# Prologue of a decoder step: the stores of memory keys, values and fold products issued from ScalarE's queue instead of SyncE's

## The chip, the core and the metric

The kernel runs on one core of one Trainium2 chip. The metric is device time in microseconds (us) of one execution, as the median of several runs. The engines are named as the profile names them: PE is TensorE (matmuls), PEld its weight loads, DVE is VectorE, ACT is ScalarE, POOL is GpSimd, and SP is SyncE, which computes nothing and here issues every transfer. A DMA is issued by an instruction in some engine's queue; the transfer itself then runs on 16 DMA engines that all queues share.

## What is computed

One layer of a decoder trunk for 2048 prompt tokens and 64 sample tokens: a combined input projection, sliding-window attention and a pooling mixer, an output projection, cross-attention into 256 memory tokens, a squared-ReLU MLP, and a final norm. All is float32 at the interface, model width 1024. The part that matters here is the memory:

```python
def _mem_kv(mem, g_mem, w_ck, w_cv):
    hm = _rmsnorm(mem, g_mem)
    k = (hm @ w_ck).reshape(B, N_MEM, N_CROSS_HEADS, CROSS_HEAD_DIM)
    v = (hm @ w_cv).reshape(B, N_MEM, N_CROSS_HEADS, CROSS_HEAD_DIM)
    return k, v
...
    q = (h @ w_cq).reshape(B, L, N_CROSS_HEADS, CROSS_HEAD_DIM)
    s = jnp.einsum('blhd,bmhd->bhlm', q, mem_k).astype(jnp.float32) * (CROSS_HEAD_DIM ** -0.5)
    p = jax.nn.softmax(s, axis=-1)
    o = jnp.einsum('bhlm,bmhd->blhd', p.astype(mem_v.dtype), mem_v).reshape(B, L, D_MODEL)
    x = x + o @ w_co
```

The memory keys and values of the prompt are also outputs.

## The kernel before

Precision comes from splitting each float32 operand in a rounded high part and a low rest, and from three matmuls per product (`mm3`, lines 108 to 113): high by high, high by low, low by high. A weight therefore passes through four steps in `Stream.emit` (lines 126 to 139): a load of 512 KB into one of six float32 buffers `f`, a cast by ACT into a high tile `w` (L136), a subtraction into a low tile `w` (L137, mostly DVE), and then the buffer is free for the next load. Twelve `w` tiles hold six weights.

The kernel has a prologue and three superblocks of 768, 768 and 576 tokens. The prologue (`prologue`, lines 368 to 452) runs once:

1. Memory keys and values: 8 + 8 weights (`in_wck`, `in_wcv`), each 24 matmuls of 256 columns. `evac` (from line 392) scales a result by the memory norm on DVE (L394), stores it to `out_mk` or `out_mv`, and splits it with `rnd` (ACT L96, DVE L97).
2. Key folds: the query weight is multiplied into the keys once, 8 weights `in_wcqt`, each giving two results of 128 x 512. `put_fold` (lines 336 to 341) copies a result from PSUM into an `f` buffer (ACT L338) and stores it to the DRAM tensor `a_s`.
3. Value folds: for each of 4 heads two weights `in_wco` give four results of 128 x 512, stored to `b_s` by the same helper.
4. The pooling weight is folded into the output weight (`prep_fold`, `fold`): the weight `in_wpool` is scaled by ACT L350 and DVE L351, and eight results go to `wo_s`. This stands between matmuls of the first superblock's input projection (L286 to L288).

Between these steps stand the first norms of the two 384-token blocks of superblock 0 (`norm1`): squares on ACT (L207, L210), their sum on POOL (L211), a column sum on PE (L220), a reciprocal root (ACT L223, L224, DVE L225 to L227), and the scaled and split activations (DVE L238, ACT L239, DVE or POOL L241).

`f` buffers are handed out when the program is written, and the copies of `put_fold` use the same six as the weight loads. In the folds, two of them serve all weight loads in turn (`f_93` and `f_96`, later `f_93` and `f_92`), and four hold results. The order of the instructions on each engine is set before the run by a scheduler that estimates durations; every engine then works its queue strictly in that order. PSUM has four buffers `mm` for these results, so a matmul group waits for the copy of the result four groups before it.

Of the kernel before, what the change touches and what calls it, by code (L numbers as in the profile page):

```python
# [51 lines left out]
def kernel(ctx: ExitStack, tc: tile.TileContext, io, nW=12, nF=6, nT=8):  # L52
    nc = tc.nc
# [37 lines left out]
    def f32(ap):  # L91
        return ap.bitcast(F32)

    def rnd(ps, hi, lo, scale=None):
        if scale is None:
            nc.scalar.copy(hi, ps)  # L96
            nc.vector.tensor_tensor(lo, ps, f32(hi), ALU.subtract)  # L97
        else:
            nc.scalar.activation(hi, ps, AF.Copy, scale=scale)
            nc.vector.scalar_tensor_tensor(lo, ps, scale, f32(hi), ALU.mult, ALU.subtract)  # L100
# [4 lines left out]
    def w8(t):  # L105
        return t[:].rearrange("p (k c) -> p k c", c=P)

    def mm3(ps, ks, Wh, Wl, Hh, Hl, first=True, final=True):
        last = len(ks) - 1
        for i, k in enumerate(ks):  # L110
            nc.tensor.matmul(ps, Wh(k), Hh(k), start=first and i == 0, stop=False)  # L111
            nc.tensor.matmul(ps, Wh(k), Hl(k), start=False, stop=False)  # L112
            nc.tensor.matmul(ps, Wl(k), Hh(k), start=False, stop=final and i == last)  # L113
# [195 lines left out]
    def flush(all_=False):  # L309
        for x in list(later):  # L310
            x[0] -= 1
            if all_ or x[0] <= 0:
                later.remove(x)
                g = x[1]()
                if g is None:
                    continue
                if all_:
                    run(g)
                elif next(g, 1) is None:
                    later.append([1, lambda g=g: g])  # L320
# [15 lines left out]
    def put_fold(ps, dsts):  # L336
        o = FS.get()
        nc.scalar.copy(o[:, 0:512], ps)  # L338
        for dst, src in dsts(o):
            nc.sync.dma_start(dst, src)  # L340
        FS.put(o)

    def prep_fold():
# [11 lines left out]
    def fold(g, wpr):  # L355
        th, tl = S.next(("wop", g))
        for eh in range(2):
            ps = MM.get()
            mm3(ps[:], [0], lambda k: wpr[:, P * g:P * g + P], lambda k: wpr[:, 512 + P * g:512 + P * g + P],
                lambda k: th[:, 512 * eh:512 * eh + 512], lambda k: tl[:, 512 * eh:512 * eh + 512])  # L360
            put_fold(ps[:], lambda o: [(wo_s[4 * eh:4 * eh + 4, :, P * g:P * g + P].rearrange("e p c -> p e c"),
                                        o[:, 0:512].rearrange("p (e c) -> p e c", c=P))])
            MM.put(ps)
        WS.put(th, tl)
        if g == 3:
            WS.put(wpr)

    def prologue():
        S.resW, S.resF = 1, 0
        mx = [XT[1][:, 0:1024], XT[1][:, 1024:2048]]  # L370
        mem = lambda k: mx[k // 4][:, 256 * (k % 4):256 * (k % 4 + 1)]
        warm = AUX.get()
        for _ in range(14):
            wu = nc.tensor.matmul(warm[:, 0:P], ones[:], ident[:], start=True, stop=True)
        AUX.put(warm)
        nc.sync.dma_start(vec[:], io["vec"])
        nc.sync.dma_start(mx[0][:, 0:512], io["mem"][:, 0:512])
        S.emit()
        hm = Act(256)
        nm = Norm(256, mem, add=nc.vector)  # L380
        for i in range(4):
            if i:
                nc.sync.dma_start(mx[i // 2][:, 512 * (i % 2):512 * (i % 2) + 512], io["mem"][:, 512 * i:512 * (i + 1)])
            for k in range(2 * i, 2 * i + 2):
                g = vec[:, V_GMEM + k:V_GMEM + k + 1]
                nc.scalar.activation(hm.hi(k), mem(k), AF.Copy, scale=g)
                nc.vector.scalar_tensor_tensor(hm.lo(k), mem(k), g, f32(hm.hi(k)), ALU.mult, ALU.subtract)
        S.emit()
        for k in range(8):
            nm.sq(k)  # L390
        S.pump()
        def evac(a, dst, c, ps):
            t = TS.get()
            nc.vector.tensor_tensor(t[:, 0:256], ps[:, 0:256], nm.r[:, 0:256], ALU.mult)  # L394
            MM.put(ps)
            nc.sync.dma_start(dst[:, 256 * c:256 * (c + 1)], t[:, 0:256])
            rnd(t[:, 0:256], a.hi(c), a.lo(c))
            TS.put(t)

        pend, outs = [], []  # L400
        for name, dst in (("ck", io["mk"]), ("cv", io["mv"])):
            a = Act(256)
            outs.append(a)
            for c in range(8):
                th, tl = S.next((name, c))
                ps = MM.get()
                if name == "ck" and c == 0:
                    with tc.issue_after(wu.ins):
                        mm3(ps[:, 0:256], range(8), lambda k: w8(th)[:, k, :], lambda k: w8(tl)[:, k, :], hm.hi, hm.lo)
                else:  # L410
                    mm3(ps[:, 0:256], range(8), lambda k: w8(th)[:, k, :], lambda k: w8(tl)[:, k, :], hm.hi, hm.lo)
                WS.put(th, tl)
                pend.append((a, dst, c, ps))
                if name == "ck" and c == FINC:
                    nm.fin()
                if name == "cv" or c >= FINC:
                    while pend:
                        evac(*pend.pop(0))
                flush()
                if (name, c) == N1C:  # L420
                    norm1(blk[0][0], N1W)
        TS.put(nm.r)
        hm.free()
        mk, mv = outs
        norm1(blk[0][1], N1Q)
        for c in range(8):
            th, tl = S.next(("cq", c))
            for hf in range(2):
                ps = MM.get()
                for h2 in range(2):  # L430
                    ks = [(hf * 2 + h2) * 2, (hf * 2 + h2) * 2 + 1]
                    mm3(ps[:, 256 * h2:256 * h2 + 256], ks, lambda k: w8(th)[:, k, :], lambda k: w8(tl)[:, k, :], mk.hi, mk.lo)
                put_fold(ps[:], lambda o: [(a_s[hf, c // 2, :, 512 * (c % 2):512 * (c % 2) + 512], o[:, 0:512])])
                MM.put(ps)
            WS.put(th, tl)
            flush()
        mk.free()
        for h in range(4):
            w = [S.next(("co", 2 * h)), S.next(("co", 2 * h + 1))]
            for mb in range(2):  # L440
                for eh in range(2):
                    ps = MM.get()
                    mm3(ps[:], range(2),
                        lambda k: mv.hi(2 * h + k, mb * P, mb * P + P), lambda k: mv.lo(2 * h + k, mb * P, mb * P + P),
                        lambda k: w[k][0][:, 512 * eh:512 * eh + 512], lambda k: w[k][1][:, 512 * eh:512 * eh + 512])
                    kt = h * 2 + mb
                    put_fold(ps[:], lambda o: [(b_s[4 * eh:4 * eh + 4, :, P * kt:P * kt + P].rearrange("e p c -> p e c"),
                                                o[:, 0:512].rearrange("p (e c) -> p e c", c=P))])
                    MM.put(ps)
                flush()  # L450
            WS.put(*w[0], *w[1])
        mv.free()
# [13 lines left out]
    def norm1(bl, wait=2):  # L466
        n = bl.n
        if bl.s == 0:
            xs = []
            load_x(bl)  # L470
            nm = Norm(n, bl.x)
        else:
            xs = [FS.get() for _ in range(4)]
            for i in range(4):
                nc.sync.dma_start(xs[i][:, 0:2 * n], io["x"][:, 8 * bl.t0 + 2 * i * n:8 * bl.t0 + 2 * (i + 1) * n])
            nm = Norm(n, lambda k: xs[k // 2][:, n * (k % 2):n * (k % 2) + n])
        for k in range(8):
            nm.sq(k)

        def rest():  # L480
            nm.fin()
            bl.h1 = Act(n)
            yield from nm.apply(V_GMIX, bl.h1.hi, bl.h1.lo, PIECE0 if bl.s == 0 else PIECE[0][bl.b])
            FS.put(*xs)

        later.append([wait, rest])
# [864 lines left out]
```

## Time and profile before

| | us |
|---|---|
| median of 3 runs | 2626.17 (2624.62 to 2628.29) |
| the profiled execution's own time | 2623.82 |
| its span, first to last instruction | 2622.0 |
| PE busy in the span | 2562.3 |
| ACT busy | 982.8 |
| DVE busy | 1300.5 |
| stores of `put_fold` | 40, of 256 KB each, issued from 67.5 to 141.4 us |
| stores of `evac` | 16, of 128 KB each, issued from 24.4 to 63.7 us |

The span and the busy times are of one profiled execution. A row of a timeline view gives start, duration, engine, line, operation, output and inputs, a count, and in brackets the idle time before it with what ended it. A waits view sums such idle times by the line that waited and the line that it waited for (total, times, longest).

### The profile page before, as it was taken

What the parts mean: (1) busy time and instruction counts of PE and PEld (TensorE: products, weight loads), DVE (VectorE), ACT (ScalarE), POOL (GpSimd) and SP (SyncE); (2) the same over time, 40 slices, a digit from 0 to 9 for tenths busy, and PEclk for the clock granted to TensorE, in tenths of its full rate; (3) what the DMA queues carried; (4) which work ended last, traced back from release to release, by engine and by line L of the source; (5) the groups of instructions that cost most, each with busy time, mean ns of one, the idle gap of its engine ahead of it and who ended that gap; (6) DMA issues with size and microseconds to landing.
All of it is one profiled execution on the core that took longest, in us unless ns stands there. A gap on an engine that the chain in (4) does not pass through costs nothing. (4 is left out here: it accounts for less than half of the span.)

```text
span 2622.0 us, 39268 instructions
## 1 busy us (share of the span) xinstructions
PE 2562.3 (98%) x15753; PEld 2457.1 (94%) x15753; DVE 1300.5 (50%) x2283; ACT 982.8 (37%) x1923; POOL 657.9 (25%) x723
## 2 busy tenths in 40 slices
PE   9899999999999999999999999999999999999998
PEld 8799989999999999897999999999999669999998
DVE  8567453533333367936363333334765645344334
ACT  6666342422222244824342222223464444322231
POOL 2215322411111152433241111113334214111111
PEclk9999999999999999999999999999999999999999
DMA  7833111211221123131111211112414572222210
GB/s 280 263 122 117 62 49 51 86 61 63 65 65 65 57 73 106 57 120 57 65 64 65 65 60 62 65 57 70 145 58 149 184 278 100 81 82 88 82 57 37
DMA packets 92539, 244.76 MB, mean 93 GB/s; under 512 B 16772, under 2 KB 31556, under 8 KB 91204
## 3 DMA queue, kind: packets, MB, share of 16 engines
q1 hardware_dynamic: 92356, 242.25, 27.9%
q8 instruction: 123, 2.02, 0.3%
q14 instruction: 60, 0.49, 0.1%
HBM read 219.53 MB, written 22.69 MB: 92 GB/s over the span
## 5 line engine op out<-in xcount | busy, mean ns | idle before, releaser
L286 PE MATMUL mm<-act,w 128*128 128x384 f32 (+2 forms) x2784 | 901.1, 324 | 2.8 <-ACT act L642 1.6
L287 PE MATMUL mm<-act,w 128*128 128x384 f32 (+2 forms) x2784 | 897.0, 322 | 3.4 <-POOL act L241 1.5
L288 PE MATMUL mm<-act,w 128*128 128x384 f32 (+2 forms) x2784 | 895.6, 322 | 1.4 <-DVE w L137 1.4
L136 ACT CAST w<-f 128x1024 fp32r<-128x1024 f32 x330 | 344.3, 1049 | 702.7 <-PE mm L112 457.6
L137 DVE TENSOR_TENSOR w<-f,w 128x1024 fp32r<-128x1024 f32 x330 | 418.4, 1276 | 305.7 <-ACT w L136 304.8
L111 PE MATMUL mm<-act,w 128*128 128x384 f32 (+2 forms) x1728 | 552.3, 320 | 2.8 <-DVE t L394 2.2
L113 PE MATMUL mm<-act,w 128*128 128x384 f32 (+2 forms) x1728 | 548.8, 318 | 1.9 <-DVE w L137 1.9
L112 PE MATMUL mm<-act,w 128*128 128x384 f32 (+2 forms) x1728 | 548.5, 317 | 0.0
L287 PEld LDWEIGHTS mm<-act,w 128*128 128x128 f32 x2784 | 525.7, 189 | 12.7 <-POOL act L241 3.7
L286 PEld LDWEIGHTS mm<-act,w 128*128 128x128 f32 x2784 | 525.8, 189 | 7.6 <-issue 2.3
L288 PEld LDWEIGHTS mm<-act,w 128*128 128x128 f32 x2784 | 525.6, 189 | 2.2 <-DVE w L137 2.0
L1144 POOL TENSOR_TENSOR t<-t 128x384 f32<-128x384 f32 (+2 forms) x192 | 216.4, 1127 | 1038.6 <-ACT t L1143 1038.6
L1177 DVE TENSOR_TENSOR x<-mm,x 128x384 f32<-128x384 f32 (+2 forms) x384 | 199.7, 523 | 327.5 <-PE mm L113 327.5
L111 PEld LDWEIGHTS mm<-act,w 128*128 128x128 f32 x1728 | 326.8, 189 | 4.7 <-ACT t L207 2.4
L113 PEld LDWEIGHTS mm<-act,w 128*128 128x128 f32 x1728 | 326.8, 189 | 2.4 <-DVE w L137 2.3
L112 PEld LDWEIGHTS mm<-act,w 128*128 128x128 f32 x1728 | 326.9, 189 | 1.1 <-issue 0.3
L211 POOL TENSOR_TENSOR t<-t,t 128x384 f32<-128x384 f32 (+2 forms) x161 | 182.2, 1132 | 337.0 <-ACT t L210 329.6
L1147 DVE TENSOR_TENSOR act<-t,act 128x384 fp32r<-128x384 f32 (+2 forms) x192 | 101.4, 528 | 295.5 <-ACT act L1146 295.4
L1146 ACT CAST act<-t 128x384 fp32r<-128x384 f32 (+2 forms) x192 | 93.5, 487 | 233.6 <-POOL t L1144 233.6
L210 ACT ACTIVATE t<-x 128x384 f32<-128x384 f32 (+2 forms) x140 | 68.0, 498 | 161.7 <-DVE x L1105 74.5
L111 PE MATMUL mm<-w,act 128*128 128x512 f32 x288 | 116.5, 407 | 9.7 <-ACT w L136 9.7
L1143 ACT ACTIVATE t<-mm 128x384 f32<-128x384 f32 (+2 forms) x192 | 88.3, 460 | 92.5 <-PE mm L288 88.6
(187 smaller groups left out, 2216.9 us busy)
## 6 DMA issues: line engine op xcount, KB each, us to landing
f<-in_wup SPq DMA_DIRECT2D x96, 512.0 KB, 3.5
f<-in_wdn SPq DMA_DIRECT2D x96, 512.0 KB, 3.5
f<-in_win SPq DMA_DIRECT2D x30, 512.0 KB, 3.8
f<-a_s SPq DMA_DIRECT2D x24, 512.0 KB, 3.5
f<-b_s SPq DMA_DIRECT2D x24, 512.0 KB, 4.7
x<-in_x SPq DMA_DIRECT2D x6, 1536.0 KB, 6.9
f<-in_wco SPq DMA_DIRECT2D x16, 512.0 KB, 5.4
f<-in_cmk SPq DMA_DIRECT2D x16, 512.0 KB, 4.3
```

Of the source, the lines that this page charges most:

```text
L111: nc.tensor.matmul(ps, Wh(k), Hh(k), start=first and i == 0, stop=False)
L112: nc.tensor.matmul(ps, Wh(k), Hl(k), start=False, stop=False)
L113: nc.tensor.matmul(ps, Wl(k), Hh(k), start=False, stop=final and i == last)
L136: nc.scalar.copy(th[:], r[:, 0:1024])
L137: eng.tensor_tensor(tl[:], r[:, 0:1024], f32(th[:]), ALU.subtract)
L211: self.add.tensor_tensor(self.acc[:, 0:n], self.acc[:, 0:n], t[:, 0:n], ALU.add)
L286: nc.tensor.matmul(ps[:, 0:n], w8(th)[:, k, :], hi(b, k), start=k == 0, stop=False)
L287: nc.tensor.matmul(ps[:, 0:n], w8(th)[:, k, :], lo(b, k), start=False, stop=False)
L288: nc.tensor.matmul(ps[:, 0:n], w8(tl)[:, k, :], hi(b, k), start=False, stop=k == 7)
L1144: nc.gpsimd.tensor_tensor(q[:, 0:n], r[:, 0:n], r[:, 0:n], ALU.mult)
L1147: nc.vector.tensor_tensor(lo, q[:, 0:n], f32(hi), ALU.subtract)
L1177: nc.vector.tensor_tensor(bl.x(m), ps[:, 0:n], bl.x(m), ALU.add)
```

## The change

All 56 stores named above are issued from ACT's queue. In `evac` the store also moves behind the split, so that it stands after ACT's cast. Nothing else is edited.

```diff
@@ put_fold
         nc.scalar.copy(o[:, 0:512], ps)
         for dst, src in dsts(o):
-            nc.sync.dma_start(dst, src)
+            nc.scalar.dma_start(dst, src)
@@ evac
             MM.put(ps)
-            nc.sync.dma_start(dst[:, 256 * c:256 * (c + 1)], t[:, 0:256])
             rnd(t[:, 0:256], a.hi(c), a.lo(c))
+            nc.scalar.dma_start(dst[:, 256 * c:256 * (c + 1)], t[:, 0:256])
             TS.put(t)
```

SP's queue falls from 509 to 453 rows and ACT's grows from 1587 to 1643. The scheduler also puts other instructions of the prologue in another order. Three places follow; in a row, the tile left of the arrow is written and those right of it are read.

The first place is ACT in the key folds, where the second block's squares meet the sixth `in_wcqt` weight (`w_85`, loaded into `f_96`). Before:

```order
L136 CAST w_85<-f_96 128x1024
L96 CAST act_72<-t_104 128x256
L210 ACTIVATE t_99<-x_106 128x384
L210 ACTIVATE t_98<-x_106 128x384
L338 COPY f_94<-mm_107 128x512
L338 COPY f_95<-mm_108 128x512
L239 CAST act_76<-t_102 128x384
L338 COPY f_91<-mm_109 128x512
L210 ACTIVATE t_104<-x_106 128x384
```

Now:

```order
L338 COPY f_94<-mm_107 128x512
L210 ACTIVATE t_104<-x_106 128x384
L340 DMA a_s<-f_94 128x512
L338 COPY f_95<-mm_108 128x512
L239 CAST act_76<-t_102 128x384
L340 DMA a_s<-f_95 128x512
L136 CAST w_85<-f_96 128x1024
L338 COPY f_91<-mm_109 128x512
L338 COPY f_92<-mm_110 128x512
```

The cast of that weight moved behind the squares, two copies and two stores; the square into `t_104` moved ahead of the copies of `f_95` and `f_91`.

The second place is ACT at the first head of the value folds. `w_85` and `w_87` are here the fourth and fifth `in_wco` weights; the copies of `mm_107` to `mm_110` ahead of the first `b_s` store are head 0's results. Before:

```order
L136 CAST w_85<-f_96 128x1024
L338 COPY f_94<-mm_107 128x512
L338 COPY f_95<-mm_108 128x512
L136 CAST w_87<-f_93 128x1024
L338 COPY f_96<-mm_109 128x512
L338 COPY f_91<-mm_110 128x512
```

Now (the first pair of copies and stores belongs to the last key fold):

```order
L136 CAST w_85<-f_96 128x1024
L338 COPY f_91<-mm_109 128x512
L338 COPY f_92<-mm_110 128x512
L340 DMA a_s<-f_91 128x512
L340 DMA a_s<-f_92 128x512
L239 CAST act_64<-t_101 128x384
L136 CAST w_87<-f_93 128x1024
L338 COPY f_94<-mm_107 128x512
L338 COPY f_95<-mm_108 128x512
L340 DMA b_s<-f_94 128x4x128
L340 DMA b_s<-f_95 128x4x128
```

Head 0's first two copies stood ahead of the cast of `w_87` and stand behind it now. In the same stretch DVE has a new order; `w_84<-f_93` is the low part of the third `in_wco` weight, whose end frees `f_93` for the fifth. Now:

```order
L137 TENSOR_TENSOR w_82<-f_96,w_81 128x1024
L241 TENSOR_TENSOR act_65<-t_97,act_63 128x384
L238 SCALAR_TENSOR_TENSOR t_103<-x_106,vec,t_99 128x384
L238 SCALAR_TENSOR_TENSOR t_104<-x_106,vec,t_99 128x384
L238 SCALAR_TENSOR_TENSOR t_101<-x_106,vec,t_99 128x384
L238 SCALAR_TENSOR_TENSOR t_100<-x_106,vec,t_99 128x384
L238 SCALAR_TENSOR_TENSOR t_98<-x_106,vec,t_99 128x384
L241 TENSOR_TENSOR act_65<-t_103,act_63 128x384
L238 SCALAR_TENSOR_TENSOR t_97<-x_106,vec,t_99 128x384
L137 TENSOR_TENSOR w_84<-f_93,w_83 128x1024
```

Before, three of these eight norm rows stood between the two L137 rows; now all eight do.

The third place is PE at the first pool fold (`w_85` here the first `in_wop` weight, `w_81` the scaled pool weight) within the second group of the input projection (`mm_110`):

```order
 L286 MATMUL mm_110<-act_63,w_83 128x384
 L287 MATMUL mm_110<-act_65,w_83 128x384
+L111 MATMUL mm_108<-w_85,w_81 128x512
+L112 MATMUL mm_108<-w_86,w_81 128x512
+L113 MATMUL mm_108<-w_85,w_81 128x512
+L111 MATMUL mm_109<-w_85,w_81 128x512
+L112 MATMUL mm_109<-w_86,w_81 128x512
+L113 MATMUL mm_109<-w_85,w_81 128x512
 L288 MATMUL mm_110<-act_63,w_84 128x384
```

The fold stood behind 19 matmuls of that group and stands behind 2 now. Behind the value folds, ACT's casts and copies go head by head: the two casts for a later head, then the four copies of a head with their stores.

## The prediction

> **What bounds the kernel now.** I read the page first, then a table by stage, then the waits of PE, of SP and of ACT in the prologue, and last the timelines around the longest waits.
>
> ```profile
> PE 2562.3 (98%) x15753; PEld 2457.1 (94%) x15753; DVE 1300.5 (50%) x2283; ACT 982.8 (37%) x1923; POOL 657.9 (25%) x723
> ```
>
> PE is busy for 98% of the span, so only time in which PE stands still can be won. The change edits the prologue alone, and its stores end at about 142 us. The table by stage has duration, busy time of each engine, granted clock, DMA share and GB/s.
>
> ```profile
> 24.50:66.00 41.50, 41.18 (x338) 40.74 (x338) 37.90 (x55) 28.17 (x52) 17.42 (x15) 1.00 0.72 245
> 66.00:88.70 22.70, 19.97 (x147) 19.33 (x148) 17.48 (x22) 16.39 (x30) 9.95 (x9) 0.92 0.77 261
> 88.70:115.70 27.00, 22.78 (x97) 17.55 (x96) 12.11 (x11) 16.22 (x27) 5.13 (x3) 1.00 0.97 279
> 115.70:127.90 12.20, 11.47 (x62) 10.61 (x61) 6.09 (x11) 8.23 (x16) 0.00 (x0) 1.00 0.86 259
> 127.90:160.00 32.10, 31.27 (x177) 29.97 (x176) 17.91 (x30) 15.48 (x25) 1.17 (x4) 1.00 0.68 220
> ```
>
> Keys and values (first row) keep PE full. The key folds (second row) lose 2.7 us, the value folds (third row) 4.2 us, and there the DMA engines are busy 97% of the time. The largest waits of PE from 24.5 to 130 us name what ended them:
>
> ```profile
> PE mm L111 <- ACT w L136: 3.5, 2, 3.0
> PE aux L220 <- POOL t L211: 2.7, 1, 2.7
> PE mm L111 <- ACT w L350: 0.7, 1, 0.7
> ```
>
> By the table PE stands still for 0.3 + 2.7 + 4.2 + 0.7 = 7.9 us up to 127.9, the most that the change can win but for a slow clock behind L220's wait, which comes below. SP waits a lot, but the question is how long it keeps loads waiting:
>
> ```profile
> SPq L340 <- ACT f L338: 17.7, 14, 3.0
> ...
> 76.78 0.80 SPq L132 DMA_DIRECT2D f<-in_wco  x1
> 81.55 0.41 SPq L132 DMA_DIRECT2D f<-in_wco  x1
> 89.93 0.33 SPq L132 DMA_DIRECT2D f<-in_wco  x1
> 97.42 0.59 SPq L132 DMA_DIRECT2D f<-in_wco  x1
> ```
>
> The 17.7 us of store waits look like loads held back. The last three rows, loads into `f_93`, tell otherwise. Each needs the end of L137 of the weight before it in that buffer:
>
> ```profile
> 79.14 1.22 DVE L137 TENSOR_TENSOR w<-f,w 128x1024 fp32r<-128x1024 f32 x1 [3.36 <-ACT w L136]
> 88.69 1.21 DVE L137 TENSOR_TENSOR w<-f,w 128x1024 fp32r<-128x1024 f32 x1
> 95.93 1.23 DVE L137 TENSOR_TENSOR w<-f,w 128x1024 fp32r<-128x1024 f32 x1 [1.02 <-ACT w L136]
> ```
>
> The ends 80.36, 89.90 and 97.16 stand against issues at 81.55, 89.93 and 97.42: SP is late by 1.2, 0.03 and 0.26 us. What the loads mostly wait for is the buffer, and that comes back over a chain of load, cast and subtraction. The casts of that chain, and its last link, the scaled pool weight:
>
> ```profile
> 94.85 1.05 ACT L136 CAST w<-f 128x1024 fp32r<-128x1024 f32 x1 [0.72 <-DMA f<-in_wco]
> 103.12 1.05 ACT L136 CAST w<-f 128x1024 fp32r<-128x1024 f32 x1 [0.75 <-DMA f<-in_wco]
> 111.26 1.05 ACT L136 CAST w<-f 128x1024 fp32r<-128x1024 f32 x1
> 118.67 1.05 ACT L136 CAST w<-f 128x1024 fp32r<-128x1024 f32 x1 [0.28 <-DMA f<-in_wop]
> 123.64 1.28 ACT L350 ACTIVATE w<-f,vec 128x128 fp32r<-128x128 f32 x4 [0.60 <-DMA f<-in_wpool]
> ```
>
> A link takes 8.27, 8.14 and 7.41 us: 2.33 from the cast's start to the end of L137, and the rest the load. The issue rows from 66 to 125 us have the time from issue to landing last:
>
> ```profile
> b_s<-f SPq DMA_DIRECT2D x16, 256.0 KB, 5.6
> ...
> f<-in_wpool SPq DMA_DIRECT2D x1, 256.0 KB, 2.6
> ...
> DMA to landing us min/median/max: 4.0/4.9/6.8
> ```
>
> The last row is of the weight loads in that stretch. So the value folds are bound by a transfer's time over two buffers, with the DMA engines nearly full.
>
> **The change part by part.** Each edit is costed with these rows.
>
> The 16 stores of keys and values. They leave SP, so the loads behind them go earlier; PE stands still for only 0.3 us in 41.5 there, so this wins at most that. On ACT each issue stands behind a cast and may run beside it. I take 0.
>
> The column sum L220. The second block's squares are added on POOL, and PE waits in order for the sum:
>
> ```profile
> 68.08 1.02 POOL L241 TENSOR_TENSOR act<-t,act 128x384 fp32r<-128x384 f32 x1
> 69.06 5.64 POOL L211 TENSOR_TENSOR t<-t,t 128x384 f32<-128x384 f32 x4
> 74.75 1.19 PE L220 MATMUL aux<-t,ones 128*128 128x384 f32 x2 [2.66 <-POOL t L211]
> 76.00:77.00 1.00, 1.00 (x6) 1.00 (x6) 0.00 (x0) 0.00 (x0) 0.63 (x1) 0.50 0.85 285
> 79.00:80.00 1.00, 1.00 (x10) 1.00 (x10) 0.86 (x1) 0.97 (x3) 0.00 (x0) 1.00 1.10 391
> ```
>
> In the new order the square into `t_104` comes earlier and that L241 behind the sums, so the last four adds can start about 1.8 us sooner (1.02 for the L241, and 0.8, my choice, for the square), at 67.2, and end at 72.9. PE waits 0.8 instead of 2.66, and the granted clock of 0.50 that follows (6 matmuls in a us against 10) should not come. Gain here: 1.9 of the wait, and about 1.1 of the slow clock. Bounds: 0 and 3.8.
>
> Its loss at head 1. The value folds' second head needs head 0's first copy to free its PSUM buffer. That copy now stands behind the cast of the fifth `in_wco` weight. The third weight's L137, which frees its buffer, now stands behind eight norm rows. They are like these:
>
> ```profile
> 82.13 1.68 DVE L238 SCALAR_TENSOR_TENSOR t<-x,vec,t 128x384 f32<-128x384 f32 x3
> ```
>
> The second weight's load goes out at 76.78 at the latest, lands 4.9 later, and cast and L137 take 2.33: 84.0. Eight rows of 0.56 are 4.5, the L137 behind them 1.2, so it ends at 89.7, as before (89.90), though its own cast is earlier. The load, issued at 89.8, lands at 94.7; the cast ends at 95.75 and the copy, 0.55, at 96.3. Head 1 began at 94.01:
>
> ```profile
> 94.01 0.39 PE L111 MATMUL mm<-w,act 128*128 128x512 f32 x1
> ```
>
> So it starts 2.3 us later, whatever was won at L220; PE has merely stood still here instead. What counts is the chain's cast, at 94.7 against 94.85.
>
> The links from there. SP's lateness is gone, 0.3 us in all, and I take the median of 4.9 for a load: three links of 2.33 + 4.9 give 116.4 for the cast that was at 118.67, 2.3 earlier. Bounds for a load: 4.0 and 6.8, the ends of that row.
>
> The issues on ACT. No trace row has a DMA issued from ACT; the nearest are SP's own (minimum, median and maximum in ns):
>
> ```profile
> L340 SPq DMA_DIRECT2D a_s<-f x16: 319/375/1132, 67.5 to 90.6; - x16
> L340 SPq DMA_DIRECT2D b_s<-f x16: 359/432/1560, 93.7 to 116.6; - x16
> ```
>
> For one head ACT has two casts (2.1), four copies (2.1 at 0.53) and four issues. At 0.43 each that is 5.9 us in a link of 7.2, which the load's flight covers. Bounds: 0.32 and 1.56 an issue; above 0.75 the cover is gone.
>
> The tail. The first matmuls of the input projection need head 3's first copy, now behind the cast at 116.4: 116.4 + 1.05 + 0.55 = 118.0, where they began at 115.72.
>
> ```profile
> 115.72 0.33 PE L286 MATMUL mm<-act,w 128*128 128x384 f32 x1
> 119.91 0.33 PE L286 MATMUL mm<-act,w 128*128 128x384 f32 x1
> 124.09 0.50 PE L111 MATMUL mm<-w,w 128*128 128x512 f32 x1 [0.72 <-ACT w L350]
> ```
>
> Twenty-four of them take 4.19, so 0.175 each. The pool fold comes after 26 of them, at 122.55; the pool weight is ready at 116.4 + 2.33 + 2.6 + 1.28 = 122.6. So the fold starts at 122.6, 1.5 earlier than 124.09, but 17 matmuls that stood ahead of it then are still to come, 3.0 us. **Sum: 3.0 - 1.5 = 1.5 us later** at the same point of the work. Behind it all is as before, and PE stood still for only 0.8 in the 32 us to 160. On the profiled execution's 2623.82 this gives 2625.3; that execution lay 2.35 below the median, so on the median's scale it is 2627.7.
>
> [...]
>
> **The rivals.**
>
> Shorter loads, faster. With stores no longer ahead of a load in its own queue, a load could take 4.0 each time. Five flights of the sum (the second weight's, the fifth's, three links) then give 4.5 back: 1.5 - 4.5 = -3.0, 2623.2 us. If PE so keeps also the 3.0 won at L220, -6.0, 2620.2 us. For it: the shortest flight in the row is 4.0. Against it: the DMA share of 0.97 with 279 GB/s. [...]
>
> ACT's queue becomes the bound, slower. If an issue from ACT takes 1.13 us, the worst of the `a_s` issues, a head costs ACT 2.1 + 2.1 + 4.5 = 8.7 against a link of 7.2: 1.5 more for each of three heads, 4.6 in all, on top of 1.5: 2632.3. It decides from 0.75 us an issue. A load of 5.6, as long as a `b_s` store, does much the same: five times 0.7 more, 2631.2. For it: full DMA engines, long issues. Against it: the median issues of 0.375 and 0.432.
>
> Nothing moves. SP's lateness was 1.5 us on this chain, most of it ahead of the place where the gain is lost. If the new order's losses and gains cancel, the time stays at 2626.2.
>
> **How the numbers follow.** A measurement of this kernel can tell about 0.2%, 5.3 us, from no change. My forecast, with the rival of nothing moved and the milder part of the others, stays within that: 0.64. Slower by more needs loads over 5.6 us or issues over a microsecond: 0.23. Faster by more needs short loads and the gain at L220 kept: 0.13. The range goes from that case, 2620.2, to loads of 5.6 (+3.5) with half of the dear issues (+2.3) on top of the sum, 2633.5.
>
> **What would show it.** Right: PE's wait at L220 under 1 us and no clock of 0.50 behind it; head 1 starting about 96 behind a cast of `in_wco`; the last cast of the chain near 116.4; the pool fold near 122.6. Wrong: weight loads landing in about 4 us from 90 to 115 us, or ACT's issues well over 0.43 us, or PE standing still in keys and values, where I have it unchanged. If the cast of `w_85`, moved back behind two stores, starved the sixth key fold, the loss would show as PE waiting for L136 near 79.

## The result and the profile after

| | before | after |
|---|---|---|
| median, us (6 runs each, on the same chip) | 2627.49 (2624.62 to 2628.50) | 2634.51 (2631.46 to 2639.16) |
| ratio | | 1.0030, 95% interval 1.0017 to 1.0043 |
| the profiled execution's own time, us | 2623.82 | 2633.56 |
| its span, us | 2622.0 | 2631.8 |

The change makes the kernel 0.3% slower, 7.0 us by the medians. The forecast was 2627.7 with a range up to 2633.5, so the result lies 1.0 beyond the range, on the side of the slower rival.

The page of the changed kernel, then its table by stage (duration, busy time of each engine, granted clock, DMA share, GB/s), with the stretches that were shown of before:

```profile
PE 2567.2 (98%) x15753; PEld 2460.3 (93%) x15753; DVE 1296.2 (49%) x2283; ACT 984.3 (37%) x1923; POOL 652.8 (25%) x723
```

```profile
24.50:66.00 41.50, 41.18 (x338) 40.74 (x338) 36.02 (x54) 27.19 (x47) 14.94 (x15) 1.00 0.69 243
66.00:88.70 22.70, 19.21 (x140) 18.54 (x141) 16.67 (x18) 16.00 (x28) 10.01 (x9) 0.92 0.74 237
88.70:115.70 27.00, 21.92 (x90) 16.66 (x89) 12.42 (x15) 17.76 (x29) 3.70 (x3) 0.94 0.86 270
115.70:127.90 12.20, 10.09 (x44) 9.12 (x43) 3.27 (x5) 5.56 (x12) 0.00 (x0) 0.86 0.74 219
127.90:160.00 32.10, 31.76 (x173) 29.75 (x172) 16.91 (x24) 17.81 (x29) 1.17 (x4) 1.00 0.81 262
```

PE now stands still for 0.3 + 3.5 + 5.1 + 2.1 = 11.0 us up to 127.9, 3.1 more than before. The clock column adds the rest: it falls below 1 in three rows instead of one. The DMA share has fallen from 0.97 to 0.86 in the value folds: the transfers are not what got scarcer. What PE waits for there is new (total, times, longest, from 24 to 130 us):

```profile
PE mm L111 <- ACT f L338: 8.8, 8, 2.6
...
PE mm L286 <- ACT f L338: 2.1, 1, 2.1
```

Before, PE waited for weights (L136) and for the norm's sum. Now it waits for ACT's copies, which free its PSUM buffers; the wait at L220 is gone. The three long ones, in PE's timeline, with the start of the pool fold behind them, and a single microsecond in the form of the stage table:

```profile
68.03 0.44 PE L111 MATMUL mm<-act,w 128*128 128x256 f32 x1 [2.30 <-ACT f L338]
...
106.21 0.79 PE L111 MATMUL mm<-w,act 128*128 128x512 f32 x1 [2.59 <-ACT f L338]
...
121.54 0.45 PE L286 MATMUL mm<-act,w 128*128 128x384 f32 x1 [2.11 <-ACT f L338]
...
128.27 0.39 PE L111 MATMUL mm<-w,w 128*128 128x512 f32 x1
```

```profile
69.00:70.00 1.00, 1.00 (x7) 1.00 (x7) 0.41 (x1) 1.00 (x2) 0.92 (x2) 0.50 0.69 262
```

Each of these waits has a stretch of 3.41 us at half clock (granted 0.50) with it, from 68.22, 105.77 and 122.83, worth 1.7 us. Three such stretches against one before (from 75.25) are two more, 3.4 us; with the 3.1 us of standing still that makes 6.5. It agrees with the pool fold: 4.2 us later than before (128.27 against 124.09), with 29 matmuls of the input projection done ahead of it instead of 43, 14 x 0.175 = 2.5 us still to come, together 6.7. Up to 160 us PE is then as full as before, and the loss stays: the same rows of DVE come 6.9 us later at 170 us and still at 1130 us. The spans of the two profiled executions differ by 9.8 us. The other 2.9 come behind 1130 us, where PE's queue has the same order in both; stretches at half clock fall at other places there. That they have to do with the change is not shown.

### The profile page after: what moved, and what is told of

It is laid out like the page before. It is cut to its first block, busy times and chain, and to the rows that moved or that the text cites. A ratio compares the mean times of both kernels' runs of the same rounds, so it can differ in the third digit from the quotient of the medians.

```text
span 2631.8 us, 39240 instructions
## 1 busy us (share of the span) xinstructions
PE 2567.2 (98%) x15753; PEld 2460.3 (93%) x15753; DVE 1296.2 (49%) x2283; ACT 984.3 (37%) x1923; POOL 652.8 (25%) x723
## 5 line engine op out<-in xcount | busy, mean ns | idle before, releaser
L136 ACT CAST w<-f 128x1024 fp32r<-128x1024 f32 x330 | 344.1, 1049 | 700.4 <-PE mm L112 455.9
L137 DVE TENSOR_TENSOR w<-f,w 128x1024 fp32r<-128x1024 f32 x330 | 418.4, 1275 | 303.1 <-ACT w L136 302.6
L111 PE MATMUL mm<-w,act 128*128 128x512 f32 x288 | 117.2, 409 | 11.3 <-ACT w L136 6.2
```

The source lines that it names most:

```text
L136: nc.scalar.copy(th[:], r[:, 0:1024])
L137: eng.tensor_tensor(tl[:], r[:, 0:1024], f32(th[:]), ALU.subtract)
```

## The experiments

Each was timed against the kernel before in the same round on the same chip, 5 to 12 runs each. "Over before" is the measured ratio less one, times 2627 us, with its 95% interval. It is not the difference of the medians: copies_first_old is 1.8 us over before by its ratio and 3.5 by its medians (2630.97 against 2627.47). So a difference of two us between two rows says little by itself.

| kernel | order of the computing | stores | median, us | over before, us |
|---|---|---|---|---|
| before | old | SP | 2626.5 to 2628.4 | |
| the change | new | ACT | 2634.51 | 7.9 (4.5 to 11.3) |
| new_order_sp | new | SP | 2641.97 | 13.1 (10.0 to 16.3) |
| old_order_act | old | ACT | 2628.52 | 0.8 (-1.6 to 3.2) |
| evac_only | scheduler's | 16 on ACT | 2629.94 | 3.2 (0.8 to 5.3) |
| fold_only | scheduler's | 40 on ACT | 2629.82 | 3.4 (1.1 to 5.5) |
| new_then_old | new, from the value folds old | ACT | 2633.91 | 5.5 (3.2 to 7.9) |
| old_then_new | old, from the value folds new | ACT | 2632.03 | 3.7 (1.3 to 5.8) |
| copies_first | new, two copies moved | ACT | 2632.98 | 5.8 (3.2 to 8.1) |
| copies_first_old | the same, from the value folds old | ACT | 2630.97 | 1.8 (-1.1 to 4.7) |
| cast_first | new, a cast moved | ACT | 2632.89 | 5.0 (2.6 to 7.4) |
| cast_copies_first | new, copies and cast moved | ACT | 2633.32 | 6.0 (3.7 to 8.4) |
| cast_copies_old | the same, from the value folds old | ACT | 2629.88 | 2.1 (0.0 to 4.5) |
| double_issue | old | ACT, folds' in halves | 2641.02 | 12.6 (9.2 to 16.0) |
| late_issue | old | ACT, issued later | 2631.31 | 3.7 (1.3 to 6.0) |
| fix_l220_sp | old, three moves | SP | 2629.00 | 0.8 (-1.3 to 3.2) |
| pool_b | old | 24 on POOL, rest SP | 2667.43 | 41.0 (37.3 to 44.7) |

### The order or the queue

The change does two things at once: it moves the issue of 56 stores, and the scheduler answers with another order on ACT, DVE, POOL and PE. Both can be parted by pinning an order: each instruction of an engine gets an added edge that says "issued behind this one" to its neighbour. So there is a kernel with the old stores and the new order, and one with the new stores and the old order. Their traces have the rows of ACT, DVE and POOL in exactly the order of the changed kernel and of the kernel before.

```python
PIN = {"Activation": [...], "DVE": [...], "Pool": [...], "PE": [...]}   # prologue, places in program order
for e, seq in PIN.items():
    ins = [...]                     # the computing instructions of engine e
    for p0, p1 in zip(seq, seq[1:]):
        tc.add_manual_dep(ins[p1], ins[p0].name, ...NoSync...)
```

> The stores stay on SP, where they were before, and ACT, DVE, POOL and PE work through the prologue in exactly the order of the changed kernel. Theory 'order' (the loss comes from where the new order puts copies, casts and squares on ACT, not from the queue that issues the stores): 4 to 9 us slower than before (the change cost 7.0), with PE waiting 6 us or more for the copies of L338 up to 130 us. Theory 'queue' (the loss comes from ACT's issue instructions, or from the stores' flights out of ACT's queue): within 2 us of before, and PE waiting under 2 us for L338.

> All 56 stores are issued by ACT, and ACT, DVE, POOL and PE work through the prologue in exactly the order of the kernel before; only the issue instructions are new on ACT. Theory 'order': within 2 us of before, PE waiting under 2 us for L338. Theory 'queue': 4 to 9 us slower than before, with PE waiting for L338 or for the squares behind slower stores. If it comes out over 2 us faster, SP's lateness was worth more than the 1.5 us that I read for it.

The order is the loss: with the old order and ACT's stores the time is that of before within the noise, with the new order and SP's stores it is 13.1 us over. PE's largest wait in each, of new_order_sp first:

```profile
PE mm L111 <- ACT f L338: 14.0, 8, 5.1
```

```profile
PE mm L111 <- ACT f L338: 3.8, 5, 1.2
```

The second meets the time that the theory of the order gave it, but not the wait: 3.8 us for copies, where under 2 were expected. The first misses what either theory gave it, by 4 us: the new order is worse with SP than with ACT. The DVE, SP, ACT and PE timelines of new_order_sp show why, around head 2 of the value folds:

```profile
95.92 1.23 DVE L137 TENSOR_TENSOR w<-f,w 128x1024 fp32r<-128x1024 f32 x1 [1.44 <-ACT w L136]
...
99.75 2.34 SPq L340 DMA_DIRECT2D b_s<-f  x4
102.19 8.35 SPq L132 DMA_DIRECT2D f<-in_wco  x3
...
107.88 2.23 ACT L136 CAST w<-f 128x1024 fp32r<-128x1024 f32 x2 [5.87 <-DMA f<-in_wco]
...
110.65 0.79 PE L111 MATMUL mm<-w,act 128*128 128x512 f32 x1 [5.11 <-ACT f L338]
```

A buffer is free at 97.15, but SP still has four stores ahead of the load, each of which waits for a copy that the new order makes late; the load goes out at 102.19, 5.0 us late, and PE stands for 5.1. So the stores' move does what it says, loads no longer wait behind them, and in the new order that is worth 5.2 us (13.1 against 7.9, with intervals that overlap by a little). In the old order, where SP was late by 1.2, 0.03 and 0.26 us, it is worth nothing that can be measured (0.8, -1.6 to 3.2).

Of the 5.0 us by which that load was late, 2.3 are the four issues (99.75 to 102.09); for the rest a store stood at the head of SP's queue and waited for its copy.

### Each edit alone

Only one of the two edits of the diff, with the order that the scheduler then makes.

> The 16 stores of keys and values on ACT, the 40 of the folds on SP. Its order on ACT has the copy of f_94 behind the squares, as in the changed kernel, and head 0's copies ahead of the fifth in_wco cast, as before. Theory 'order': the first part of the loss, 1.5 to 3.5 us, with PE standing still near 68 us for the first fold buffer. Theory 'queue' with the issues of the folds as the cost: within 1 us of before. Theory 'queue' with slower landing of out_mk and out_mv as the cost: 2 to 5 us.

> The 40 stores of the folds on ACT, the 16 of keys and values on SP. Its order on ACT has the fold copies ahead of the square into t_104, and head 0's copies behind the fifth in_wco cast, as the changed kernel has. Theory 'order': no gap near 68 us, the later part of the loss stays, 3 to 5.5 us. Theory 'queue': the whole 7 us if the folds' issues are the cost, within 1 us if the flights of out_mk and out_mv are.

Both came out where the theory of the order had them, 3.2 and 3.4 us. The waits of PE from 66 to 130 us, of evac_only first:

```profile
PE mm L111 <- ACT w L350: 3.2, 1, 3.2
PE mm L111 <- ACT f L338: 3.1, 1, 3.1
```

```profile
PE mm L111 <- ACT f L338: 5.0, 4, 2.4
PE aux L220 <- POOL t L211: 2.7, 1, 2.7
PE mm L286 <- ACT f L338: 2.5, 1, 2.5
```

evac_only has the one wait near 68 us and none for copies in the value folds; fold_only has the waits in the value folds and the old wait at L220. The gap of evac_only comes though its fold copies' stores are on SP, so ACT's issues of fold stores don't make it. Slower landing of `out_mk` and `out_mv`, for which the text above gives 2 to 5 us, would fit the 3.2 us as well; but old_order_act has the same 16 stores on ACT and is at before, so it isn't that. The wait for the pool weight (L350) in evac_only was expected by neither theory, and how much of the 3.2 us is due to it is open.

### Which part of the order

The orders differ in many rows, on ACT from 24.8 us on. PE's waits point at two places. At the first, ACT's copy of `f_94` stands behind squares. In ACT's timeline of the changed kernel, and DVE's at the same time:

```profile
66.56 0.94 ACT L210 ACTIVATE t<-x 128x384 f32<-128x384 f32 x2 [3.08 <-issue]
67.41 0.56 ACT L338 COPY f<-mm 128x512 f32<-128x512 f32 x1
```

```profile
61.98 2.06 DVE L137 TENSOR_TENSOR w<-f,w 128x1024 fp32r<-128x1024 f32 x1
63.97 1.23 DVE L97 TENSOR_TENSOR act<-t,act 128x256 fp32r<-128x256 f32 x1
65.12 1.36 DVE L241 TENSOR_TENSOR act<-t,act 128x384 fp32r<-128x384 f32 x1
```

The square needs `t_99`, which that L241 frees at 66.48; in the new order it stands behind L137 and L97. The page names no releaser ("issue"), but the square starts 0.08 us behind the end of L241. These three rows are also long. In both kernels every L137 up to 160 us with nothing on POOL beside it takes 1.21 to 1.23 us, such an L97 0.29 to 0.56, such an L241 0.55 or 0.56. Here they take 2.06, 1.23 and 1.36, 2.3 us or more above that, which is as much as PE's gap. POOL's sums run beside them (first row, of the changed kernel); in the kernel before an L137 at the like place falls between two of those sums, with only a copy of 15 columns beside it (second row):

```profile
63.21 2.86 POOL L211 TENSOR_TENSOR t<-t,t 128x384 f32<-128x384 f32 x2 [0.24 <-ACT t L210]
61.91 1.21 DVE L137 TENSOR_TENSOR w<-f,w 128x1024 fp32r<-128x1024 f32 x1
```

That POOL's work is what lengthens them was not tested. At the second place, two casts of weights stand ahead of each head's first copy (ACT, head 1's copies in the third row, head 3's in the last):

```profile
102.45 1.05 ACT L136 CAST w<-f 128x1024 fp32r<-128x1024 f32 x1 [0.99 <-DMA f<-in_wco]
104.63 1.04 ACT L136 CAST w<-f 128x1024 fp32r<-128x1024 f32 x1 [1.12 <-DMA f<-in_wco]
105.58 1.06 ACT L338 COPY f<-mm 128x512 f32<-128x512 f32 x2
...
119.95 1.04 ACT L136 CAST w<-f 128x1024 fp32r<-128x1024 f32 x1 [1.69 <-DMA f<-in_wop]
120.91 1.07 ACT L338 COPY f<-mm 128x512 f32<-128x512 f32 x2
```

The cast at 104.63 is of the seventh `in_wco` weight, which head 3 will use; head 2 has to wait for it, at 106.21, because its PSUM buffers are freed by copies that stand behind it in ACT's queue. The two places were parted with the pinned orders, all stores on ACT; the cut takes in all of the order ahead of it or behind it, not the rows above alone. In words:

```diff
-PIN: the new order                                         (the changed kernel)
+PIN: new up to the sixth key weight's copies, old behind   (new_then_old)
+PIN: old up to there, new behind, PE's order included      (old_then_new)
```

> All stores on ACT. Each engine works in the changed kernel's order up to the sixth key-fold weight's copies (the squares ahead of the copy of f_95, POOL's sums ahead of its L241), and from there in the order of the kernel before: the casts of the value-fold weights stand between a head's copies again, not ahead of them. Measured so far: the whole new order on ACT stores is about 7 us over before, the whole old order on ACT stores about 1.4. Theory 'casts ahead of copies' (the loss is in the value folds): 1 to 4 us over before, PE waiting under 4 us for L338 behind 88 us. Rival 'the squares at 68 us start it' (a first delay shifts every later load): 5 to 7 us.

> The mirror: all stores on ACT, the order of the kernel before up to the same point, and the changed kernel's order behind it, with two casts of value-fold weights ahead of each head's first copy. Theory 'casts ahead of copies': 4 to 7 us over before, PE waiting for L338 at the starts of heads 1, 2 and 3 and of the input projection, 5 us or more in all. Rival 'the squares start it': 1 to 2.5 us, and no wait over 1 us at heads 2 and 3.

Over old_order_act that is 4.7 us for the first place and 2.9 for the second. The first fell on the rival's side (5 to 7), the second just under what my theory gave it (4 to 7). So both parts of the order cost, and neither explains all; for the second this pair's intervals overlap (1.3 to 5.8 and -1.6 to 3.2), and the pairs below bear it out. Then the first place was repaired, alone and together with the second (ACT's rows):

```diff
 L210 ACTIVATE t_102<-x_106
+L338 COPY f_94<-mm_107
+L338 COPY f_95<-mm_108
 L210 ACTIVATE t_98<-x_106
 L210 ACTIVATE t_99<-x_106
 L210 ACTIVATE t_97<-x_106
-L338 COPY f_94<-mm_107
 L210 ACTIVATE t_104<-x_106
-L338 COPY f_95<-mm_108
```

> The changed kernel with one move on ACT: the copies of f_94 and f_95 stand ahead of the three squares into t_98, t_99 and t_97 instead of behind them. In the changed kernel those squares start at 66.56, when DVE's L241 has freed t_99, and the copy behind them leaves PE standing for 2.3 us and then at half clock for 3.4 us (1.7 us lost). Theory 'copies behind waiting squares are the first part of the loss': no gap at 68 us, and 2.5 to 4 us faster than the changed kernel (so 3 to 4.5 over before), as far as it isn't given back. If the value folds take it back (they wait for loads anyway): within 1.5 us of the changed kernel, 5.5 to 8 over before.

> Both repairs in one: all stores on ACT, the new order with those two copies moved ahead of the squares, and the order of the kernel before in the value folds (casts between a head's copies). Theory 'the order is the loss': 1.5 us over before or less, with L220's gain kept down to 2 us faster than before. If something else in the first part of the new order costs (DVE's order, the squares ahead of the fifth copy): 4 us or more over before, as without the moved copies (6.5 by medians).

The gap at 68 us and its half clock go in both (cast_copies_old below, with the same copies ahead, has the clock at 1.00 from 66 to 88.7 us). With the old order behind it, this gives back 3.7 us (5.5 to 1.8, intervals that overlap), close to what was expected; with the new one it is taken back in good part (7.9 to 5.8, intervals that overlap too). Could the late cast of `w_85` be what takes it back?

```diff
+L136 CAST w_85<-f_96          (ACT; its L137 on DVE two rows up)
 L96 CAST act_72<-t_104
 ...
-L136 CAST w_85<-f_96
 L338 COPY f_91<-mm_109
```

> The changed kernel with w_85's cast on ACT moved up to where it stood before (ahead of the last L96 of the values) and its L137 on DVE moved up by two rows; nothing else. Theory 'late f_96': the loads into f_96 go 3 to 6 us earlier, and the time is 1 to 4 us less than the changed kernel's, though the gap at 68 us grows by the 1.2 us of the L137 that now stands ahead of the L241 it waits for. Rival 'the value folds' order alone sets the end': within 1.5 us of the changed kernel.

> Both moves of the first part: w_85's cast early, and the copies of f_94 and f_95 ahead of the squares; the value folds in the new order. Theory 'late f_96 took the repair back': 2 to 5 us faster than the changed kernel, so 2.5 to 5 over before, which is what the value folds' order costs (old order first, new order then: 3.7). Rival: as copies_first, 5.8 over before.

> The same two moves, and the value folds in the order of before; all stores on ACT. If these three places are the whole loss: from 1 us over before down to 3 us faster, since L220's wait is gone too. If ACT's issues keep costing: 1.5 to 3 us over before.

Hardly. The last key weight's load went out at 66.6 and 66.5 instead of 73.0, as expected. The cast alone came to 5.0, 2.9 less than the change's 7.9 and within what that theory gave it, but with intervals that overlap; with the copies ahead as well, the cast gains nothing (6.0 against 5.8 without it). What the three kernels with the new order in the value folds have in common is their waits for copies there; the largest waits of PE behind 60 us, of cast_copies_first and of cast_copies_old:

```profile
PE mm L111 <- ACT f L338: 10.2, 8, 2.8
PE mm L286 <- ACT f L338: 2.0, 1, 2.0
```

```profile
PE mm L111 <- ACT f L338: 5.0, 5, 1.6
```

So what the key folds win, the new order of the value folds takes: 5.8 against 1.8, and 6.0 against 2.1. In these two pairs that order is worth about 4 us by the ratios, and by the medians, which were taken in the same round, 2.0 and 3.4; the two pairs further up have 2.4 (7.9 against 5.5) and 2.9. Each pair's intervals overlap, but all four lie on the same side. The last kernel also stands where its text has it if ACT's issues keep costing (1.5 to 3 us): old_order_act, at 0.8, shows no such cost, and the intervals don't decide.

### ACT's issues

The changed kernel's issues took no longer than SP's (ns, minimum, median, maximum):

```profile
L340 ACTq DMA_DIRECT2D a_s<-f x16: 326/326/567, 68.0 to 94.3; - x16
L340 ACTq DMA_DIRECT2D b_s<-f x16: 366/438/1275, 97.8 to 124.5; - x16
```

Whether they are covered was asked by doubling them in the old order, and by moving each away from its copy (the second edit is told in words):

```diff
 for dst, src in dsts(o):
-    nc.scalar.dma_start(dst, src)
+    nc.scalar.dma_start(dst[0:64], src[0:64])
+    nc.scalar.dma_start(dst[64:128], src[64:128])
```

> The old order with all stores on ACT, but each of the 40 fold stores is issued as two of 64 partitions: 40 more issue instructions on ACT of 0.33 to 0.44 us, 15 us more in all, for the same bytes. If ACT's issues run beside its computing and are covered: within 2 us of the kernel with old order and ACT stores (which was 1.4 over before). If they hold up the copies, as the 3.8 us of waits for L338 there suggest: 3 to 8 us over before, with the waits for L338 at twice that or more.

```diff
-L338 COPY, L340 DMA of it, L338 COPY, L340 DMA of it
+L338 COPY, two computing instructions, L340 DMA of it     (late_issue, PIN with the DMAs in it)
```

> All stores on ACT and the old order of all computing, as in the kernel that came out 1.4 us over before; but each of the 40 fold stores is issued behind the second computing instruction after its copy, not directly behind the copy, so that ACT's queue does not stand until the copy is done. Theory 'an issue directly behind its copy holds ACT's queue' (about 0.4 us a pair, as the trace of the changed kernel shows ahead of the L239 at 91.27): 1 to 4 us faster than with the old order and ACT stores, so 0.5 to 3 us faster than before. Rival 'an issue costs ACT its own 0.33 to 0.44 us wherever it stands': no difference to it, 0 to 3 us over before. If stores that start later hold result buffers too long, it is slower, and PE waits for L338 that wait for stores.

Doubling costs 11.8 us over old_order_act, more than forecast. The two halves of a store, and PE's waits:

```profile
L340 ACTq DMA_DIRECT2D a_s<-f x16: 452/453/1676, 68.1 to 100.9; - x16
...
L341 ACTq DMA_DIRECT2D a_s<-f x16: 606/609/647, 68.7 to 101.4; - x16
```

```profile
PE mm L111 <- ACT f L338: 7.8, 14, 1.5
```

A half takes longer than the whole took (0.45 and 0.61 us against 0.33), so a store costs ACT 1.06 us. That is above the 0.75 us from which the prediction said that cover is gone, and its price was right in kind: issues of a microsecond would have made the kernel slower. At 0.33 to 0.44, in the old order, no cost can be measured.

late_issue gained nothing at the end: 3.7 us over before, 0.8 for old_order_act, with intervals that overlap. Its first matmul of the input projection started 2.4 us earlier than in old_order_act, but then PE waited for the pool weight, at half clock behind it (granted 0.91 from 115.7 to 127.9 us):

```profile
115.53 0.33 PE L286 MATMUL mm<-act,w 128*128 128x384 f32 x1
...
126.26 0.79 PE L111 MATMUL mm<-w,w 128*128 128x512 f32 x1 [3.09 <-ACT w L350]
```

So whether the place of an issue matters stays open.

### Can anything be won here

> The kernel before with its stores on SP and all its orders, but for three moves ahead of L220: POOL adds the squares ahead of its L241, DVE does the last L97 of the memory values a row earlier, ACT squares into t_104 behind the copy of f_95. This is the gain that the prediction gave to L220, alone. If it reaches the end: 2 to 3.5 us faster than before. If the value folds, bound by their loads, take it back (the prediction's reading): within 1 us, with L220's wait at 1 us or less and longer waits for L136 at heads 1 to 3.

The three moves were made with everything else pinned as before, SP's queue too. It came out at before (0.8, -1.3 to 3.2), but not cleanly: L220's wait fell only to 1.9 us, and a wait of 1.6 for the copies at 68.81 came in its place, so it doesn't tell the two theories apart.

```diff
-def put_fold(ps, dsts):
+def put_fold(ps, dsts, eng=nc.gpsimd):     # a_s: eng=nc.sync; order of before pinned
...
-    nc.sync.dma_start(dst, src)
+    eng.dma_start(dst, src)
```

> The kernel before with its orders, but the 24 stores of b_s and wo_s are issued by POOL, which computes little between 88 and 140 us; the others stay on SP. Loads are then held back by no b_s store, and ACT issues nothing. If the store waits on SP, or the stores' place ahead of the loads, are worth something in the old order: 1.5 to 4 us faster than before. If the value folds only wait for buffers and transfers (the prediction's reading): within 1.5 us. If issues from POOL are slow or land late, PE waits for copies that wait for stores: over 3 us slower.

41 us slower. POOL's issues, and what ACT's copies wait for from 66 to 128 us:

```profile
106.16 0.75 POOL L340 DMA_DIRECT2D b_s<-f  x1 [2.37 <-issue]
109.19 0.76 POOL L340 DMA_DIRECT2D b_s<-f  x1 [2.27 <-issue]
```

```profile
ACT f L338 <- DMA b_s<-f: 17.6, 8, 4.2
```

At best one store in 3.0 us leaves POOL, where a link of the chain with its four stores took 7.4 to 8.3 before, and the four result buffers fill up. No kernel here beats the kernel before.

## Why the prediction was wrong, step by step

**The bound.** Right in part: the loss is made in the prologue, and behind 128 us PE is as full as before up to 160. But standing still is only 3.1 us of it; 3.4 are PE at half clock.

**The stores of keys and values: 0.** No cost of the issues was seen, but the edit has one: with it alone the new order comes at 68 us, 3.2 us over before.

**L220.** The wait went, as forecast (0 instead of 0.8). But I took the earlier squares as free. The step "the square into `t_104` comes earlier ... so the last four adds can start about 1.8 us sooner" looked at the sums behind the squares, not at the copy of `f_94`, which in the new order stands behind three of them (their rows are in the diff of copies_first). PE waited 2.3 us for that copy and ran 3.4 us at half clock, so L220 ran at 75.38 instead of 74.75: 0.6 later where I had it 1.9 earlier. The slow clock behind L220, which I took as 1.1, was too small as well: 3.4 us at half clock are worth 1.7. old_order_act and copies_first_old show that this was the order: with the copies ahead, the first place costs nothing that can be measured.

**Head 1.** Right in mechanism: copies stand behind the cast of the fifth weight, and that weight is late behind eight norm rows. The size was off. "The second weight's load goes out at 76.78 at the latest" failed: it went at 79.4, since the cast of `w_85` had moved back. I priced only whether that move starves the sixth key fold (it didn't, here), not what its buffer loads next. The fifth weight's load went out at 92.68 instead of 89.8; its flight of 3.6 us, 1.3 shorter than the 4.9 that I took, gave part of that back. Its cast was at 96.28 instead of 94.7, and head 1 began at 97.87 instead of 96.3, 1.6 late.

**The links.** The median load got shorter, as the faster rival had it, yet not in the chain. The weight loads from 66 to 125 us, and the three that carry the chain's last links:

```profile
DMA to landing us min/median/max: 3.6/4.0/6.0
...
L132 SPq DMA_DIRECT2D f<-in_wco x2: 328/328/328, 98.0 to 98.6; - x2
DMA to landing us min/median/max: 6.0/6.0/6.0
L132 SPq DMA_DIRECT2D f<-in_win x1: 328/328/328, 107.0 to 107.0; - x1
DMA to landing us min/median/max: 5.1/5.1/5.1
L132 SPq DMA_DIRECT2D f<-in_wop x1: 332/332/332, 114.4 to 114.4; - x1
DMA to landing us min/median/max: 5.4/5.4/5.4
```

6.0, 5.1 and 5.4 against the 4.9 that I took are 1.8 us of the 2.0 by which the three links were longer (23.67 us from 96.28 to 119.95, forecast 21.7). A head's four stores are issued around each of these loads; whether that is what lengthened them was not tested.

**The tail.** 119.95 + 1.05 + 0.55 = 121.55, and the first matmul of the input projection is at 121.54: the rule held, 3.5 us later than forecast. Here is the step that was missing: PE's waits at the starts of heads 2 and 3 and of the input projection were in my times, the half clock behind them was not. I had priced it at L220 and nowhere else. The one behind 121.54 adds 1.7. The step from 26 matmuls to "17 matmuls that stood ahead of it then are still to come" was off by three: the section on the change has the fold behind 2 matmuls of the second group, the trace has it behind 24 + 5 = 29 in all. With 3.5 + 1.7 the fold is 5.2 later than forecast, and 128.27 against 122.6, 5.7, less 3 x 0.175 for the three that no longer follow, is 5.1. So of what the sum lacked, 1.6 us are head 1, 2.0 the links, and 1.7 the half clock that was put at nothing, to a tenth or two of rounding. The forecast's 1.5 and these 5.1 make 6.6 us at the pool fold of one execution, near the 7.0 between the medians.

**The rivals.** "ACT's queue becomes the bound" gave 2632.3 and was nearest to the time, but not for its reason: the issues took 0.33 to 0.44 us by their medians, and with the old order they cost nothing that can be measured. What ACT's queue did was to tie PE's buffers to weight loads. "Shorter loads" was right about the median (4.0) and wrong about the end. "Nothing moves" is, within 0.8 us (-1.6 to 3.2), what the stores' move alone gives.

What stays open: how much of the first place is the gap and how much the late weights behind it, since the value folds' order covers both; how much of the gap is the length of DVE's rows beside POOL's; whether some 2 us of ACT's issues remain; and why evac_only, late_issue and copies_first_old wait 3 us for the pool weight.

## What to carry to other kernels

A DMA moved to a computing engine's queue is not one edit but a new order on every engine that the scheduler then makes: pin the old order once and time the two apart, before the transfers are blamed. In an order, look at each copy that frees a buffer of the engine that bounds the kernel, and ask what the rows ahead of it wait for; a prefetch cast ahead of such a copy makes the bound engine wait for a load that it needs only much later (2.59 us here, at 106.21). And price the half clock behind every wait that an edit adds, as a chance (here 9 of 15 waits of 2 us and more had it, at 1.7 us each), not only behind the one that it removes.

## What the runs showed of the hardware that was not expected

- A stretch of 3.41 us at half clock (granted 0.50) came with 9 of the 15 waits of PE of 2 us and more in the profiled executions of before and of the changed kernel; it began between 0.6 us ahead of the wait's end and 1.3 us behind it. One came with a shorter wait, 1.47 us (the changed kernel at 1978.28). In old_order_act and in cast_copies_old the clock was 0.94 from 88.7 to 115.7 us, which is about one stretch, and PE's longest wait from 66 to 130 us was 1.6 us. None came with the 2.97 us at 110.93 of before. Within each of the two executions, before and changed, the stretches start a whole number of 3.41 us apart: in the changed kernel's prologue at 68.22, 105.77 and 122.83, 11 and 5 times 3.41 us. Near 26 us it is a matter of chance: in 12 profiled executions PE waits 2.2 to 2.5 us at the first results of the memory keys, and from 26 to 27 us the clock is 0.50 in 5 of them (new_order_sp, fold_only, new_then_old, double_issue, cast_first) and 1.00 in the others. The same microsecond of new_then_old and of the changed kernel:

```profile
26.00:27.00 1.00, 1.00 (x7) 1.00 (x6) 0.96 (x3) 0.74 (x2) 0.00 (x0) 0.50 0.98 352
```

```profile
26.00:27.00 1.00, 1.00 (x10) 1.00 (x10) 0.73 (x3) 0.78 (x2) 0.03 (x1) 1.00 0.98 382
```

  A stretch came with waits of 1.5 to 2.6 us and not with one of 2.97, so what sets it off is not shown. One stretch more or less is 1.7 us, so an edit of a few us is timed over many runs.
- The second of two issues in a row on ACT, each of half an `a_s` store, took 0.61 us, the first 0.45 (double_issue, medians), where one whole store took 0.33 (the changed kernel).
- POOL's issues took 0.75 us, but one store left at best every 3.0 us (pool_b).
- DVE's L137 took 1.21 to 1.23 us in each of 63 rows up to 160 us that had nothing on POOL beside them, in the kernel before and the changed one, and up to 2.06 us in rows that had.
